# A two-layer diffusion backbone on one core: layer 0's projections written out in one order

## The chip, the core and the metric

The kernel runs on one core of a Trainium2 chip. A core has five engines that this text speaks of by their names in the profile: TensorE (PE, matmuls; its weight loads are listed as PEld), VectorE (DVE), ScalarE (ACT), GpSimd (POOL) and SyncE (SP, which here issues most DMAs). Each works through its own queue of instructions in order and waits on semaphores for the others. The metric is the time of one execution on the device in microseconds (us).

## The reference

The program computes two layers of a diffusion backbone over 1024 latent tokens and 256 context tokens of width 1024, in float32. Layer 0 is grouped-query attention (16 query heads, 4 key/value heads of 64), layer 1 is latent attention. The change touches only what layer 0 does ahead of its attention:

```
shift, scale, gate = split(silu(c) @ w_mod + b_mod, 3)          # and the same for c_ctx
h  = rms_norm(x, norm_w) * (1 + scale) + shift                   # 1024 x 1024; hc: 256 x 1024
k, v, q, g = split(h @ w_in, [256, 512, 1536])                   # 2560 columns; hc @ w_in too
q = rope(rms_norm(q per head, q_norm));  k = rope(rms_norm(k per head, k_norm))
o = softmax(q k^T / 8) v                                          # latent rows read all keys, context rows context keys
y = (o * silu(g)) @ w_out
```

## The kernel before, in words

The 1280 tokens are ten tiles of 128 rows (tiles 0 to 7 latent, 8 and 9 context), handled in five pairs. The 1024 channels are eight slices of 128, KT = 8.

*Modulation.* `mod_sections` (L197) computes silu(c) @ w_mod for one third of w_mod (a section: shift, scale or gate) and one half of the 1024 columns at a time: eight loads `mraw` of 128 x 512, and eight matmuls (L222) with 32 columns of the condition, `s32`, as the stationary operand; four neighbouring ones write four different strips of 32 partitions of one PSUM bank `pm`. `rows` copies the bank to SBUF (L228), and `end` folds it and puts it into columns A (scale) and B (shift), four channel slices for each half.

*Modulated rows.* `load_pair` (L709) loads two tiles `xt` and normalizes them (`norm_rows`: squares on ScalarE, root on GpSimd L118, scaling on VectorE). `modulate` (L278) takes two channel slices of a pair at a time: four transposes on TensorE into a PSUM bank `tp` (L288), the affine step `hmod` = tp * A + B on VectorE in two instructions of 128 x 256 (L292), the high part `hh` by a copy on ScalarE (L296), and the low part `hl` = hmod - hh on GpSimd or VectorE (L135). Each matrix is held as a high and a low part, and `mm3` (L88 to L94) forms each product from three matmuls per channel slice: high x high, low x high, high x low.

*Weights.* `load_weight` (L137) brings 1024 x 512 columns of w_in in four pieces `wraw` (L152), through three buffers, and splits each into `wa` (ScalarE, L156) and `wb` (GpSimd or VectorE, L135). There are two such pairs in a ring, so that one projection is used while the next is loaded. The order is keys and values (kv), queries in two chunks (q0, q1), gates in two chunks (g0, g1).

*Tiles.* A kv or query tile is 24 matmuls of 128x512 into one PSUM bank `mm`. `head_norm` (L776) follows: squares on ScalarE (L781), sums on VectorE, the root `h_rs` on GpSimd (L118), rope gains on VectorE and an addition on GpSimd, scaling by the root on VectorE (L800, tile `t`). Then `head_store` (L803): transposes (L808), the split, two stores.

*The order.* A scheduler of the language orders the instructions on each engine; `in_order` pins the order of TensorE alone, and only for the first modulation sections and x tiles 0 and 1. `staged` runs the transposes of a tile after the products of the next. The first half of the channel slices of tiles 0, 1 and 2 is multiplied early (`begun`), while the second half of the modulation is still being loaded. Then come kv tiles 0 to 9, q0 of tiles 0 to 9, q1 of tiles 0 to 9, the gates g0 (`gate_path`, four m of 128 gate channels, each over 512, 512 and 256 tokens), and then attention, beside which g1 is done. Between the products of the queries the modulation for later (the gate section of layer 0 and all of layer 1) is worked in, one step for every two channel slices, with its loads two steps ahead.

The pools of PSUM: three banks for products, three for transposes, two for modulation. All loads and stores go by SP's queue. The lines that set the order:

```
735    load_pair(0)                                    # pinned on TensorE
738    wkv = load_weight(w_in0, KT, 0, 512)
834    staged(range(TT), kv_stage, lambda tt, kn: head_store(kn, 4, tt, k0h, k0l, 0))
836    wq0 = load_weight(w_in0, KT, 512, 512)
856    wq1 = load_weight(w_in0, KT, 1024, 512)
857    q_chunk(0, wq0)
858    q_chunk(1, wq1)
860    wg0 = load_weight(w_in0, KT, 1536, 512)
```

## Time and profile before

| what | us |
|---|---|
| three runs | 1788.57, 1781.73, 1786.39; median 1786.39 |
| profiled execution, its own time | 1781.91 |
| span of that execution (all in the trace) | 1780.1 |
| mean granted clock of TensorE | 0.989 |
| first product of layer 0 starts | 27.19 |
| kv tile 5 done | 91.7 |
| last kv product, queries begin | 119.8 |
| queries and modulation done | 278.7 |
| gates g0 done, all that is rewritten ends | 332.5 |

The profile is one execution. Busy time is listed for each engine; a stage table gives it for stretches of the span, with the clock that TensorE was granted as a share of full speed. The list of waits says which engine stood idle at which line, and which instruction released it. In the timeline a matmul's shown duration runs over the next one's start, so the pace is read from the starts. A modulation matmul of the trace counts as x2, so x8 are four of them.

### The profile page before, as it was taken

What the parts mean: (1) busy time and instruction counts of PE and PEld (TensorE: products, weight loads), DVE (VectorE), ACT (ScalarE), POOL (GpSimd) and SP (SyncE); (2) the same over time, 40 slices, a digit from 0 to 9 for tenths busy, and PEclk for the clock granted to TensorE, in tenths of its full rate; (3) what the DMA queues carried; (4) which work ended last, traced back from release to release, by engine and by line L of the source; (5) the groups of instructions that cost most, each with busy time, mean ns of one, the idle gap of its engine ahead of it and who ended that gap; (6) DMA issues with size and microseconds to landing.
All of it is one profiled execution on the core that took longest, in us unless ns stands there. A gap on an engine that the chain in (4) does not pass through costs nothing.

```text
span 1780.1 us, 23773 instructions
## 1 busy us (share of the span) xinstructions
PE 1729.4 (97%) x8392; PEld 1224.1 (69%) x8392; DVE 1055.3 (59%) x1803; ACT 638.3 (36%) x943; POOL 978.5 (55%) x654
## 2 busy tenths in 40 slices
PE   7899999999999999999989999999999999999999
PEld 3676667885656565547878899987666666666587
DVE  3664543256777777734565667756666666666232
ACT  2431212104545444452234543331344344434410
POOL 2554431207888887873235554351677777776611
PEclk8999999999999999999999999999999999999999
DMA  8555765422242423227433776777254443533352
GB/s 288 174 157 183 233 195 164 136 71 76 66 124 66 107 71 72 72 69 216 126 109 102 207 222 167 192 210 209 51 126 103 107 106 84 119 87 74 94 170 74
DMA packets 220782, 235.01 MB, mean 132 GB/s; under 512 B 34040, under 2 KB 162792, under 8 KB 220664
## 3 DMA queue, kind: packets, MB, share of 16 engines
q1 hardware_dynamic: 220664, 233.50, 46.9%
q8 instruction: 66, 1.08, 0.3%
q14 instruction: 52, 0.43, 0.1%
HBM read 159.51 MB, written 73.63 MB: 131 GB/s over the span
## 4 chain that ended last, share of the span: by engine, by line
PE 81%; DVE 4%; POOL 3%; DMA 3%; issue 3%; ACT 1%; SPq 0%; POOLq 0%; ACTq 0%; DVEq 0%
PE st L442 21%; PE av L478 16%; PE mx L379 7%; PE mm L92 6%; PE mm L94 6%; PE mm L93 6%; PE y L92 3%; PE y L94 3%; PE y L93 3%; PE mx L384 2%; PE av L524 1%; PE pm L222 1%; DMA wraw<-in_l_w_in 1%; PE tp L808 1%; DVE wb L135 1%
## 5 line engine op out<-in xcount | busy, mean ns | idle before, releaser
L444 ACT ACTIVATE p<-st 128x1024 f32<-128x1024 f32 x328 | 335.7, 1026 | 369.4 <-PE st L442 195.8
L380 DVE TENSOR_REDUCE m<-mx 128x1 f32<-128x512 f32 x512 | 351.1, 690 | 159.0 <-PE mx L379 155.3
L465 POOL TENSOR_TENSOR acp<-acp,p 128x1024 f32<-128x1024 f32 x127 | 301.9, 2377 | 104.8 <-ACT p L444 100.7
L478 PE MATMUL av<-p,v 128*64 128x512 f32 x1312 | 296.5, 597 | 0.0
L478 PEld LDWEIGHTS av<-p,v 128*64 128x64 f32 x1312 | 88.1, 136 | 174.9 <-issue 170.1
L451 DVE TENSOR_REDUCE acd<-p 128x512 f32<-128x1024 f32 x126 | 150.3, 1234 | 23.5 <-ACT p L444 23.5
L386 DVE TENSOR_REDUCE m<-mx 128x2 f32<-128x512 f32 x144 | 99.2, 692 | 99.6 <-PE mx L384 99.0
L135 POOL TENSOR_TENSOR wb<-wraw,wa 128x512 fp32r<-128x512 f32 (+3 forms) x69 | 91.0, 1333 | 112.5 <-ACT wa L156 112.3
L465 POOL TENSOR_TENSOR acp<-acp,acd 128x1024 f32<-128x1024 f32 x63 | 149.8, 2377 | 4.2
L465 POOL TENSOR_TENSOR acp<-p 128x1024 f32<-128x1024 f32 x35 | 83.7, 2391 | 121.4 <-ACT p L444 118.0
L92 PE MATMUL mm<-wa,hh 128*128 128x512 f32 (+2 forms) x336 | 128.3, 382 | 2.5 <-ACT hh L296 2.5
L442 PE MATMUL st<-QH,KL 96*128 96x512 f32 x320 | 123.2, 392 | 0.0
L94 PE MATMUL mm<-wa,hl 128*128 128x512 f32 (+2 forms) x336 | 122.9, 367 | 0.0
L93 PE MATMUL mm<-wb,hh 128*128 128x512 f32 (+2 forms) x336 | 122.8, 366 | 0.0
L92 PE MATMUL y<-wa,oh 128*128 128x512 f32 x288 | 113.0, 392 | 2.2 <-ACT oh L642 2.2
L94 PE MATMUL y<-wa,ol 128*128 128x512 f32 x288 | 111.9, 390 | 0.6 <-DVE x_ms L116 0.6
L93 PE MATMUL y<-wb,oh 128*128 128x512 f32 x288 | 112.1, 389 | 0.0
L442 PE MATMUL st<-QA,KA 128*128 128x512 f32 x336 | 106.8, 399 | 0.9 <-ACT p L444 0.8
L442 PE MATMUL st<-QB,KB 65*128 65x512 f32 x336 | 105.5, 395 | 0.0
L379 PE MATMUL mx<-KA,QA 128*128 128x512 f32 x256 | 103.7, 410 | 0.4 <-DVE m L380 0.3
L379 PE MATMUL mx<-KH,QH 96*128 96x512 f32 x256 | 103.3, 406 | 0.8 <-DVE m L380 0.8
L92 PE MATMUL mm<-hh,wa 128*128 128x512 f32 x256 | 101.3, 396 | 0.3 <-ACT th L85 0.3
(208 smaller groups left out, 3326.4 us busy)
## 6 DMA issues: line engine op xcount, KB each, us to landing
mraw<-in_l_w_mod SPq DMA_DIRECT2D x96, 256.0 KB
wraw<-in_l_w_in SPq DMA_DIRECT2D x28, 512.0 KB
rb<-rrow SPq DMA_DIRECT2D x72, 128.0 KB
xt<-in_x SPq DMA_DIRECT2D x16, 512.0 KB
wraw<-in_l_w_out SPq DMA_DIRECT2D x16, 512.0 KB
sgd<-gth SPq DMA_DIRECT2D x32, 256.0 KB
QA<-q0h SPq DMA_DIRECT2D x32, 256.0 KB
sg<-sgd SPq DMA_DIRECT2D x64, 128.0 KB
```

The source lines that it names most:

```text
L92: pe.matmul(ps, lhsT=lh(k), rhs=rh(k), start=first and i == 0, stop=False)
L93: pe.matmul(ps, lhsT=lh(k), rhs=rl(k), start=False, stop=False)
L94: pe.matmul(ps, lhsT=ll(k), rhs=rh(k), start=False, stop=last and i == len(ks) - 1)
L135: eng.tensor_sub(lo, a, b)
L379: pe.matmul(m, lhsT=s["mq"][:, i * P:(i + 1) * P], rhs=s["mk"][:, n * 512:(n + 1) * 512], start=True, stop=True)
L380: dve.reduce_max(s["m"][:, i, n:n + 1], m, axis=AX.X)
L386: dve.reduce_max(s["m"][:, 2 * i:2 * i + 2, 2 if u["kind"] == "lat" else 0], m.rearrange("p (a b) -> p a b", a=2), axis=AX.X)
L442: pe.matmul(ps[:, n * 512:(n + 1) * 512], lhsT=lh, rhs=rf(n), start=(j == 0), stop=(j == len(prods) - 1))
L444: act.activation(p, ps, AF.Exp, scale=self.ops["scale"])
L451: dve.reduce_sum(t[:, ns], p2.rearrange("p a n -> p n a")[:, ns, :], axis=AX.X)
L465: pool.tensor_add(t, a, b)
L478: pe.matmul(s["av"][64 * n:64 * n + 64, :], lhsT=s["v"][:, kt, u["vc"]:u["vc"] + 64], rhs=p[:, n * 512:(n + 1) * 512], start=kt == kts[0], ...
```

## The change

The order of everything from the start to the first two m of g0 is now written out. A list `Plan` takes functions with a due time, sorts them and issues them with the order of all five engines pinned (TensorE, ScalarE, VectorE, GpSimd, SP). The unit of time is a quarter tile: the products of two channel slices, six matmuls.

- kv of tiles 0 to 5, then q0 of tiles 0 to 5, kv of tiles 6 to 9, q0 of tiles 6 to 9, q1 of tiles 0 to 9, m 0 and 1 of g0. m 2 and 3 follow outside of the plan by `gate_slice`, as before. For tiles 0 to 3 the first halves come first, then the second halves.
- `hmod`: of its two instructions the first one (pairs 0 to 2) or both (pairs 3 and 4) are on ScalarE as an affine activation.
- Loads: the modulation's first sections, x tiles 0 and 1, two kv weight pieces, x tiles 2 and 3, the rest of the modulation, the last two kv pieces, tables, x tiles 4 and 5, and so on. The six small loads of condition and bias rows are issued by ScalarE's queue.
- The modulation matmuls stand in groups of four. The loads of a group are issued when the group three ahead is done.
- PSUM: four banks for products, three for transposes, one for modulation. Six work buffers from the start (before: five for keys, six for queries).

The diff, cut to its core:

```diff
-    def mod_sections(which, pool_of, bufs, rowp, ps_mod, ps_tp, lag):
...
+    class ModHalf:
...
+        def load(self, k):
+            c0 = self.sec * D + self.half * 512
+            self.st[k] = self.pool_of().tile([P, 512], F32, name="mraw", tag="mraw", bufs=self.bufs)
+            sp.dma_start(self.st[k], ins[f"l{self.l}_w_mod"][k * P:(k + 1) * P, c0:c0 + 512])
+
+        def mult(self, i):
+            st = self.st
+            if i == 0:
+                st["pm"] = self.ps_mod.tile([P, 512], F32, name="pm", tag="pm")
+            for q in range(4 * i, 4 * i + 4):
+                c = 32 * (q % 4)
+                pe.matmul(st["pm"][c:c + 32, :], lhsT=s32[:, q, :], rhs=st.pop(q), start=q < 4, stop=q >= 4)
...
+    class Plan:
...
+        def at(self, t, fn, *args):
+            self.todo.append((t, len(self.todo), fn, args))
+
+        def run(self):
+            engines = mybir.EngineType
+            with tc.manual_schedule(engines={engines.PE, engines.Activation, engines.DVE, engines.Pool, engines.SP}):
+                for _, _, fn, args in sorted(self.todo, key=lambda e: e[:2]):
+                    fn(*args)
...
-    ps_mm = stP.enter_context(tc.tile_pool(name="psmm0", bufs=3, space=PSUM, reuse_waits="tile"))
+    ps_mm = stP.enter_context(tc.tile_pool(name="psmm0", bufs=4, space=PSUM, reuse_waits="tile"))
...
-    ps_mod = stT.enter_context(tc.tile_pool(name="psmod0", bufs=2, space=PSUM, reuse_waits="tile"))
+    ps_mod = stT.enter_context(tc.tile_pool(name="psmod0", bufs=1, space=PSUM, reuse_waits="tile"))
...
+    def mod_group(pair, g, t, ts, on_act, low, d=0.45):
...
+        def scale():
+            st["h"] = wk.tile([P, 512], F32, name="hmod", tag="w512")
+            for kk in range(2):
+                k = 2 * g + kk
+                dst, src = (v[:, kk * 256:(kk + 1) * 256] for v in (st["h"], st["t"]))
+                a, b = A[0][:, k, cond:cond + 1], Bv[0][:, k, cond:cond + 1]
+                if kk < on_act:
+                    act.activation(dst, src, AF.Identity, scale=a, bias=b)
+                else:
+                    dve.tensor_scalar(dst, src, a, b, op0=ALU.mult, op1=ALU.add)
...
+        plan.at(t, turn)
+        plan.at(ts, scale)
+        plan.at(ts + d, cast)
+        plan.at(ts + 2 * d, rest)
...
+    def finish_tile(nm, tt, e, nh, tabset, dst_h, dst_l, pair0, late=0):
...
+        wide = nh > 4
+        plan.at(e + 0.05, squares)
+        if nm == "kv":
+            plan.at(e + 0.7, v_store)
+        plan.at(e + 0.4, gains)
+        plan.at(e + (3.0 if wide else 2.2), scale)
+        plan.at(e + (4.5 if wide else 3.9), turn)
+        plan.at(e + (4.8 if wide else 4.2), parts)
+        plan.at(e + (5.4 if wide else 4.9), store)
...
+    def mod_loads(b):
+        if b < 8:
+            for k in range(4 * (b % 2), 4 * (b % 2) + 4):
+                halves[b // 2].load(k)
+
+    def mod_mult(b):
+
+        halves[b // 2].mult(b % 2)
+        mod_loads(b + 3)
+
+    plan.at(-50, lambda: rows.update(cond=cond_load(), cols=cols_load()))
...
+    weight("kv", 0, -48, (-47.5, -47, 5.2, 5.5), (-40, -39, 6.05, 7.2))
...
+    mod_group(1, 0, 2.6, 2.65, 1, dve, 0.1)
+    mod_group(1, 1, 3.3, 3.35, 1, dve, 0.1)
+    for tt in range(4):
+        for i in range(2):
+            plan.at(2 * tt + i, products, "kv", tt, i)
+            plan.at(8 + 2 * tt + i, products, "kv", tt, 2 + i)
+    for b, t in ((4, 1.5), (5, 2.5), (6, 4.4), (7, 5.6)):
+        plan.at(t, mod_mult, b)
...
+    for g in range(4):
+        mod_group(2, g, 12.5 + g, 12.9 + g, 1, (dve, pool)[g % 2])
+        mod_group(3, g, 25.5 + 3 * g, 26.2 + 3 * g, 2, pool)
+        mod_group(4, g, 38.5 + 2 * g, 39.2 + 2 * g, 2, pool)
...
+    slot = 16
+    for tts in (range(6), range(6, TT)):
+        for tt in tts:
+            if tt >= 4:
+                for i in range(4):
+                    plan.at(slot + i, products, "kv", tt, i)
+                slot += 4
+                kv_tile(tt, slot)
+        for tt in tts:
+            q_tile(0, tt, slot)
+            slot += 4
...
+    at_step = 47.6
+    for l, sec in ((0, 2), (1, 0), (1, 1), (1, 2)):
+        for half in range(2):
+            mh = ModHalf(l, sec, half, lambda: mp[0], 8, wk, ps_mod, ps_tp)
+            for k in range(KT):
+                plan.at(at_step + k, mh.load, k)
+            for b in range(2):
+                plan.at(at_step + 4 * b + 6.1, mh.mult, b)
...
+    for m in range(2):
+        for s0 in range(0, NT, 512):
+            slot = gate_tile(0, m, s0, slot)
+    plan.run()
...
-        gate_path(0, 0, wg0, hT, NT, ps_mm, wkg)
+        for m in range(2, 4):
+            for s0 in range(0, NT, 512):
+                gate_slice(0, 0, m, s0, min(512, NT - s0), ws["g0"], hT, ps_mm, wkg)
```

Three places of the instruction streams show what moves. The first is TensorE's queue in the first products (`mm`), where the second half of the modulation (`pm`) is worked in. Before:

```order
L92 MATMUL mm_318<-wa_246,hh_131 128x512
L222 MATMUL pm_280<-mraw_272,s32_117 32x512
L92 MATMUL mm_305<-wa_246,hh_131 128x512
...
L93 MATMUL mm_305<-wb_247,hh_131 128x512
L222 MATMUL pm_280<-mraw_274,s32_117 32x512
L94 MATMUL mm_305<-wa_246,hl_132 128x512
...
L93 MATMUL mm_318<-wb_247,hh_131 128x512
L222 MATMUL pm_280<-mraw_276,s32_117 32x512
L94 MATMUL mm_318<-wa_246,hl_132 128x512
```

and now:

```order
L94 MATMUL mm_326<-wa_169,hl_118 128x512
L198 MATMUL pm_339<-mraw_212,s32_122 32x512
L198 MATMUL pm_339<-mraw_214,s32_122 32x512
L198 MATMUL pm_339<-mraw_216,s32_122 32x512
L198 MATMUL pm_339<-mraw_218,s32_122 32x512
L92 MATMUL mm_352<-wa_169,hh_117 128x512
...
L94 MATMUL mm_352<-wa_169,hl_118 128x512
L198 MATMUL pm_339<-mraw_270,s32_122 32x512
L198 MATMUL pm_339<-mraw_272,s32_122 32x512
L198 MATMUL pm_339<-mraw_274,s32_122 32x512
L198 MATMUL pm_339<-mraw_276,s32_122 32x512
```

Before, single modulation matmuls stand between the products of tiles 0 and 1 (`mm_305`, `mm_318`) as the scheduler placed them; now four stand together behind the first twelve products of tile 0 (`mm_326`), and four more behind the first six of tile 1 (`mm_352`).

The second is TensorE's queue where keys give way to queries: `mm_1098` and `mm_787` are the last kv products, `wa_1155` and `wa_478` the high part of the query weights, `t1` the normalized keys. Before:

```order
L93 MATMUL mm_1098<-wb_247,hhc_443 128x512
L94 MATMUL mm_1098<-wa_246,hlc_444 128x512
L808 MATMUL tp_1137<-ident_70,t1_1083 128x128 x2
L92 MATMUL mm_1238<-wa_1155,hh_131 128x512
...
L94 MATMUL mm_1238<-wa_1155,hl_132 128x512
L808 MATMUL tp_1146<-ident_70,t1_1131 128x128 x2
L92 MATMUL mm_1238<-wa_1155,hh_131 128x512
```

and now:

```order
L94 MATMUL mm_787<-wa_169,hl_118 128x512
L879 MATMUL tp_859<-ident_70,t1_811 128x128 x2
L92 MATMUL mm_862<-wa_478,hh_117 128x512
...
L94 MATMUL mm_862<-wa_478,hl_118 128x512
L756 MATMUL tp_898<-ident_70,xt_551 128x128
L756 MATMUL tp_898<-ident_70,xt_553 128x128
...
L92 MATMUL mm_862<-wa_478,hh_117 128x512
...
L94 MATMUL mm_862<-wa_478,hl_118 128x512
L879 MATMUL tp_921<-ident_70,t1_883 128x128 x2
L92 MATMUL mm_924<-wa_478,hh_117 128x512
```

Before, the transposes of tile 8 stand right behind the last product of tile 9, and those of tile 9 twelve products on; now those of tile 4 stand behind tile 5, those of tile 5 24 products on, and transposes of later x tiles (`xt`) lie between.

The third is SP's queue at the start, with the semaphores that an entry waits for (one of each DMAHW number stands for a DMA slot). Before, from its 25th row:

```order
L212 DMA mraw_229<-in_l0_w_mod 128x512 [waits DMAHW7_49,PE_49]
L152 DMA wraw_248<-in_l0_w_in 128x2x512 [waits DMAHW0_49]
L152 DMA wraw_254<-in_l0_w_in 128x2x512 [waits DMAHW1_49]
L152 DMA wraw_260<-in_l0_w_in 128x2x512 [waits DMAHW2_49]
L212 DMA mraw_272<-in_l0_w_mod 128x512 [waits DMAHW3_49,PE_49]
L152 DMA wraw_266<-in_l0_w_in 128x2x512 [waits DMAHW0_49,DMAHW4_49,DVE_49,Pool_49]
L212 DMA mraw_274<-in_l0_w_mod 128x512 [waits DMAHW5_49,PE_49]
L212 DMA mraw_276<-in_l0_w_mod 128x512 [waits DMAHW6_49,PE_49]
L212 DMA mraw_278<-in_l0_w_mod 128x512 [waits DMAHW7_49,PE_49]
```

and now, from its 11th row:

```order
L726 DMA xt_167<-in_x 128x1024 [waits DMAHW7_49]
L152 DMA wraw_171<-in_l0_w_in 128x2x512 [waits DMAHW0_49]
L152 DMA wraw_173<-in_l0_w_in 128x2x512 [waits DMAHW1_49]
L190 DMA mraw_175<-in_l0_w_mod 128x512 [waits DMAHW2_49]
...
L190 DMA mraw_350<-in_l0_w_mod 128x512 [waits DMAHW3_49,PE_49]
L152 DMA wraw_420<-in_l0_w_in 128x2x512 [waits DMAHW4_49]
L152 DMA wraw_422<-in_l0_w_in 128x2x512 [waits DMAHW5_49,DVE_49,Pool_49]
L791 DMA cw_k_429<-in_rope_cos0 128x8x64 [waits DMAHW6_49]
```

Before, the fourth weight piece, which waits for VectorE and GpSimd, stands ahead of three modulation loads and of x tiles 2 and 3; now two pieces stand ahead of the modulation's second half, and the two others behind all of it.

## Rows read from the trace of the kernel before

**Rows 1.** The profile page, part 1: busy time of each engine

```profile
PE 1729.4 (97%) x8392; PEld 1224.1 (69%) x8392; DVE 1055.3 (59%) x1803; ACT 638.3 (36%) x943; POOL 978.5 (55%) x654
```

**Rows 2.** Table by stage: us, busy by engine, granted clock, DMA share, GB/s

```profile
0.00:27.20 27.20, 16.79 (x59) 5.67 (x59) 6.05 (x17) 5.58 (x10) 3.44 (x12) 0.80 0.75 262
27.20:54.20 27.00, 24.72 (x109) 13.17 (x109) 13.44 (x24) 8.82 (x16) 8.58 (x10) 0.95 0.69 229
54.20:92.00 37.80, 32.10 (x153) 25.53 (x153) 31.37 (x76) 21.39 (x46) 22.31 (x24) 0.95 0.65 206
92.00:119.80 27.80, 27.00 (x131) 22.00 (x130) 16.72 (x46) 9.32 (x24) 13.92 (x16) 1.00 0.37 106
119.80:140.00 20.20, 16.19 (x61) 12.63 (x60) 11.22 (x19) 4.72 (x9) 11.19 (x9) 0.83 0.65 208
140.00:278.70 138.70, 135.31 (x674) 92.75 (x673) 70.07 (x138) 30.04 (x54) 56.40 (x39) 1.00 0.64 198
278.70:332.50 53.80, 53.80 (x276) 46.22 (x275) 10.81 (x16) 7.62 (x14) 1.61 (x2) 0.97 0.47 138
```

**Rows 3.** List of waits, TensorE, 0 to 332.5 us: total, times, longest

```profile
PE tp L808 <- DVE t L800: 8.2, 6, 2.7
PE tp L288 <- DVE hmod L292: 5.8, 4, 3.7
```

**Rows 4.** Timeline, TensorE, 116 to 146 us: start, duration, engine, line, operation, [idle before]

```profile
122.93 0.66 PE L808 MATMUL tp<-ident,t 128*128 128x128 f32 x2 [2.74 <-DVE t L800]
...
124.67 0.63 PE L92 MATMUL mm<-wa,hh 128*128 128x512 f32 x1
...
128.51 0.63 PE L92 MATMUL mm<-wa,hh 128*128 128x512 f32 x1
...
129.45 0.39 PE L92 MATMUL mm<-wa,hh 128*128 128x512 f32 x1
...
132.89 0.39 PE L92 MATMUL mm<-wa,hh 128*128 128x512 f32 x1
```

**Rows 5.** Timeline, TensorE: the modulation matmuls, at 31 and at 151 us

```profile
30.99 1.05 PE L222 MATMUL pm<-mraw,s 128*32 128x512 f32 x2
31.96 0.50 PE L92 MATMUL mm<-wa,hh 128*128 128x512 f32 x1
...
151.01 1.07 PE L222 MATMUL pm<-mraw,s 128*32 128x512 f32 x8
```

**Rows 6.** Groups by line and shape, 27-140 us: busy, mean ns, idle

```profile
L292 DVE TENSOR_SCALAR hmod<-tp,A,B 128x256 f32<-128x256 f32 x37 | 17.8, 539 | 0.8 <-PE tp L288 0.6
L135 POOL TENSOR_TENSOR wb<-wraw,wa 128x512 fp32r<-128x512 f32 x11 | 15.4, 1407 | 15.8 <-ACT wa L156 15.8
...
L118 POOL TENSOR_TENSOR h_rs<-h_ms,mhalf 128x4 f32<-128x4 f32 x10 | 10.9, 1094 | 14.0 <-DVE h_ms L116 13.9
...
L781 ACT ACTIVATE sq<-mm 128x256 f32<-128x256 f32 x10 | 3.8, 383 | 11.5 <-PE mm L94 11.5
```

**Rows 7.** Timeline, TensorE, 278 us: the last transposes of the queries

```profile
278.04 0.63 PE L808 MATMUL tp<-ident,t 128*128 128x128 f32 x4 [1.93 <-DVE t L800]
```

**Rows 8.** Timeline, queue of SP, 0 to 60 us

```profile
18.56 0.34 SPq L212 DMA_DIRECT2D mraw<-in_l_w_mod  x1
27.62 0.37 SPq L152 DMA_DIRECT2D wraw<-in_l_w_in  x1
```

**Rows 9.** Table by stretches of 4 us, columns as in rows 2

```profile
12.00:16.00 4.00, 3.45 (x14) 1.81 (x14) 0.66 (x2) 0.00 (x0) 0.00 (x0) 0.62 0.83 287
...
20.00:24.00 4.00, 3.22 (x10) 0.49 (x6) 1.45 (x2) 1.14 (x2) 0.78 (x2) 0.60 1.03 389
24.00:28.00 4.00, 2.70 (x18) 2.36 (x19) 2.84 (x7) 1.48 (x3) 0.75 (x2) 0.83 0.10 37
```

**Rows 10.** Timeline, TensorE, 4 us: the first modulation matmuls

```profile
4.28 5.10 PE L222 MATMUL pm<-mraw,s 128*32 128x512 f32 x8 [1.39 <-DMA mraw<-in_l_w_mod]
```

**Rows 11.** Chain of waits, 0 to 500 us: start, duration, what it is

```profile
200.93 4.18 DMA wraw<-in_l_w_in
```

More of the change, by code (lines that the diff above doesn't have):

```diff
@@ L750, in hybrid_kernel @@
[L750 to L761 removed]
+    wk = stR.enter_context(tc.tile_pool(name="wk0", bufs=6, **right))
@@ L858, in hybrid_kernel, with weight, alloc, products @@
-    q_chunk(1, wq1)
-    drain(mods)
-    wg0 = load_weight(w_in0, KT, 1536, 512)
+    ws = {}
+    def weight(nm, c0, begin, loads, splits):
+        pieces, held = [], []
+        def alloc():
+            ws[nm] = load_weight(w_in0, KT, c0, 512, 2, todo=pieces)
+        plan.at(begin, alloc)
+        for i in range(4):
+            plan.at(loads[i], lambda: held.append(pieces.pop(0)()))
+            plan.at(splits[i], lambda i=i: held[i]())
+    acc = {}
+    def products(nm, tt, i):
+        if i == 0:
+            acc[nm, tt] = ps_mm.tile([P, 512], F32, name="mm", tag="mm")
+        lh, ll = h_cols(hT, tt)
+        w = ws[nm]
+        mm3(acc[nm, tt], lh, ll, lambda k: w[0][:, k, :], lambda k: w[1][:, k, :], range(2 * i, 2 * i + 2), i == 0, i == 3)
@@ new lines, in hybrid_kernel @@
+    rows = {}
+    halves = [ModHalf(0, sec, half, lambda: mp[0], 12, wk, ps_mod, ps_tp) for half in range(2) for sec in range(2)]
+    def mod_loads(b):
[7 more added lines that the diff above has]
+    for b in range(2):
+        plan.at(-49, mod_loads, b)
+    for tt in range(2):
+        plan.at(-48, x_load, tt)
```

457 lines of the change are left out of this document (253 added, 204 removed).

## The prediction

> **What bounds the kernel now.** I read the page first: TensorE is busy 97% of the span [rows 1], so only what takes time away from TensorE can move the end, and the question is where it idles or runs slowly. The table by stage [rows 2] answers that for the part that is rewritten, which ends at 332.5 us, when the first four gate channels are done. From 27.2 us on TensorE idles 27.0 - 24.7 = 2.3 us in the first products, 5.7 in the key/value tiles up to 92 us, 0.8 up to 119.8, 4.0 at the change to the queries, 3.4 in the 138.7 us of queries and modulation, and nothing in the gates: 16.2 us together. Before 27.2 us it waits for loads; there the loads bound it. The list of waits [rows 3] names what ends the idle time: mostly the transposes of normalized keys and queries (L808), which wait for VectorE, and the transposes of x (L288), which wait for a PSUM buffer that the affine step `hmod` on VectorE holds. VectorE is busy 31.4 us of 37.8 in the stage from 54.2 to 92 us [rows 2]; no other engine is so near its limit there.
>
> Two more losses are not idle time. The granted clock is 0.83 in the stage 119.8 to 140 and 0.97 in the gates [rows 2]. In the trace the products after the 2.7 us wait at 122.9 start every 3.84 / 9 = 0.427 us and later every 3.44 / 15 = 0.229 us [rows 4]: the two levels, 1.2 and 2.4 GHz. And the modulation of the second half of the channels runs matmul by matmul as its loads land: one matmul (which the trace counts as x2) holds TensorE from 30.99 to 31.96, 0.97 us, while four together (x8), which write four different strips of 32 partitions, take 1.0 us [rows 5].
>
> **The change, part by part.** The arithmetic stays: as many products, transposes and modulation matmuls. So the sum is over what surrounds them.
>
> (1) *Waits that go.* In the new order a tile's transposes stand about four quarter-tiles behind its last product (a quarter tile is 6 products, 6 x 0.229 = 1.37 us), so 5.4 us for keys and over 6 us for queries, and there is always another tile's product in between, also where keys give way to queries and queries to gates. Before, the wait at 122.9 us came because the 1.09 us root on GpSimd stood behind a 1.41 us split of query weights [rows 6], and only 12 products lay in between. I take all 16.2 us as removable, and put new waits in (4).
>
> (2) *Slow clock that goes with them.* At 119.8 to 140: 13 products at 0.427 instead of 0.229, 2.6 us. In the gates: granted 0.97 over 53.8 us, so 0.03 x 2 x 53.8 = 3.2 us at the low level, half of it lost: 1.6; it follows the 1.9 us wait at 278.0 [rows 7]. At 54.2 to 92: 0.05 x 2 x 37.8 = 3.8 us at the low level, of which part is the 3.7 us wait itself; I count 1.0. Together 5.2. The low clock of the first products (0.95 over 27.0 us, 1.4 us lost) follows the wait for loads and stays.
>
> (3) *Modulation in fours.* Of the 16 matmuls of the second half five stand alone, 5 x (0.97 - 0.25) = 3.6 us more than in fours; two and three together take about as long as four, which adds about 0.7 by the same rows. 4.3 us go, if all four loads are there. They should be: before, the queue of loads stood still from 18.56 to 27.62 us [rows 8], because the fourth weight piece waited for a buffer, and the DMA engines fell to 37 GB/s [rows 9]. Now that piece stands behind all the modulation loads. Their 4 MB follow on 7 MB, so at 0.38 MB/us they land from about 25 to 36 us, each group of four ahead of the quarter tile in which it is used (31 to 44 us by adding up the new order).
>
> (4) *New waits.* The written order holds five queues at once; a late instruction holds all behind it. The tight place is tiles 0 to 5 of the keys. Of the 40 affine pieces 28 go to ScalarE, where the nearest rows are the squares of the same shape, 0.383 us against 0.539 on VectorE [rows 6]. In the stage from the second half of tile 0 to the end of tile 5 there are 16 pieces (before, 22, all on VectorE, together with the fourth pair of x): VectorE falls from 31.4 to 31.4 - 14 x 0.54 = 23.8 us, and ScalarE rises by 8 x 0.38 = 3.1 to at most 24.5, in a stage that should now last about 31 us. So none is full, but each waits for the others in turn. By hand I followed the four queues here and found three places: the first low parts (0.8 us), the third pair's transposes, since its loads are issued only when the first pair's last transposes are done, 1.2 us, and the last quarter of tile 4, which waits for its affine step behind the three tiles' norms on VectorE, and for the low part on GpSimd, 2 us. That is 4; with what I have missed I take 5. Bounds: 0, if the engines overlap as their busy times allow, and 11.4, twice what the same kind of work loses now. For the rest, where each tile leaves the other engines half idle (VectorE 70 of 138.7 us), 1.5.
>
> The Trainium skill speaks against the affine step on ScalarE: ScalarE: Activation LUTs, section on what ACT_TABLE_LOAD costs, gives 0.186 us plus 0.83 ns per element and about 0.093 us more for each operand that is a column of per-partition values. The row agrees for the squares without such a column (0.186 + 0.213 = 0.40 against 0.383); for two columns an estimate from that page is 0.586 us, longer than VectorE's 0.539. By it ScalarE would rise 1.6 us more in the tight stage and the sum below would be at most 1.6 smaller. No row here shows such a step on ScalarE.
>
> (5) *The start.* The first product needs both first-half modulation sections. Before, 5.2 MB of loads stood ahead of their last piece, now 6.3 MB: two weight pieces come first. At 389 GB/s [rows 9] that is 2.7 us later. Against it the six small loads go to ScalarE's queue: of eight loads that may be under way four were of 4 to 12 KB there, and from 12 to 16 us the rate was 287 GB/s [rows 9], which at 389 would save about 2 us over 8 us. Then half the affine step is beside the other (0.5 us). I take 0, between -3 and +3. ScalarE's tanh now stands behind its six load issues, one of which waits for the first modulation piece, so the first modulation matmul starts later than 4.3 us [rows 10]; the loads still set the pace up to 9 us, so this costs nothing unless ScalarE is later than that.
>
> (6) *Four buffers of PSUM for products, one for modulation*: the next modulation group starts two quarter tiles behind the copy of the one before; nothing. From the first maxima on the order of TensorE's queue is unchanged, so what is gained by 332.5 us is kept to the end.
>
> Sum: 16.2 + 5.2 + 4.3 = 25.7 go, 5 + 1.5 = 6.5 come: 19.2 us. The profiled execution took 1781.9 us (span 1780.1): 1762.7. The median of the runs shown lies 4.5 us above it, which gives 1767.2. I predict 1765, between the two.
>
> **The rivals.** (A) *The tight stage gives much of it back.* Mechanism: VectorE, ScalarE and GpSimd in one written order wait in turn, each key tile's chain for the last; every wait above 2 us brings some 2 us of slow clock [rows 4]. Upper bound 11.4 us for (4), with two restarts of 2.6: the gain falls to 19.2 - 6.4 - 5.2 = 7.6, 1777. For it: GpSimd's slow pieces (1.41 and 1.09 us) lie in the chain of every key tile. Against: busy times of about 24 in 31 us.
>
> (B) *The loads' queue makes it slower.* Stores and modulation loads share SP's queue in one order, and a store waits there until its tile is split; everything behind waits too. If each of the 16 later modulation groups met its loads 2 us late, 32 us would be lost against 19 gained: 1778 + 17 = about 1795, also where queries now run with no load waited for. It decides from 1.2 us a group. Against: a group's last load is issued 3.1 quarter tiles ahead of its matmuls, at least 4.3 us, and a load of twice the size took 4.2 us from issue to landing [rows 11].
>
> (C) *The start costs its 2.7 us* and the small loads bring nothing: 16.5 us, 1768; it is inside the forecast's range.
>
> (D) *The order is held without any new wait*: 25.7 - 1.5 = 24 us, and 2 at the start: 1757.
>
> By the skill's price alone: 1766.6.
>
> **How the numbers follow.** Forecast (gain 12 to 24 us, with C): 0.68, own range 1759 to 1774. A: 0.17. B: 0.05. D: 0.10. The range that leaves out 2 in 10 reaches from D to A: 1755 to 1779. A difference of 0.5%, 8.9 us, is what can be told from no change: faster needs less than 1777.5. Forecast and D are faster throughout, and a quarter of A: 0.82; the rest of A: 0.13; B: 0.05.
>
> **What would show it.** In the changed profile: the first product at 26 to 29 us; modulation matmuls in groups of x8 with no wait for their loads; the gate's first four channels done at about 313 us instead of 332.5; TensorE idle from the first product to there about 6 us, most of it before tile 5 is done, ended by VectorE, ScalarE or GpSimd; granted clock 1.0 from 80 us on; no idle time where queries begin and where gates begin. Wrong if TensorE waits for `mraw` loads during the queries (B), if the first product comes after 31 us, if it idles over 10 us before tile 5 is done (A), or if the time after the gates is not the same as before.

## The result and the profile after

The changed kernel took 1771.74 us (median of 4 runs, 1770.01 to 1774.55), the kernel before 1785.76 (4 runs, 1781.73 to 1788.57) beside it: a ratio of 0.9925, 95% interval 0.9899 to 0.9950, so 13 to 14 us faster. The forecast was 1765, with 1755 to 1779 as its range. The gain has the right sign and some two thirds of the size; the time lies about halfway between the forecast and rival A's 1777.

The page's first line now, which answers to [rows 1]:

```profile
PE 1715.4 (97%) x8392; PEld 1218.4 (69%) x8392; DVE 1054.3 (60%) x1771; ACT 651.6 (37%) x971; POOL 985.2 (56%) x658
```

TensorE is as full as before, in a span that is 11.9 us shorter. The table by stage, with stretches that fit the new order: to the first product, the first halves of tiles 0 to 3, to the end of key tile 5, to the end of the early queries' waits, and to the end of the first four m of the gates:

```profile
0.00:27.04 27.04, 13.18 (x58) 5.50 (x58) 7.99 (x17) 7.27 (x13) 5.08 (x13) 0.83 0.92 333
27.04:48.50 21.46, 21.41 (x110) 14.12 (x111) 7.40 (x14) 7.61 (x14) 2.38 (x3) 0.89 0.78 247
48.50:85.30 36.80, 29.05 (x132) 20.81 (x130) 28.46 (x61) 22.35 (x48) 26.50 (x29) 1.00 0.59 172
85.30:112.00 26.70, 22.99 (x114) 18.67 (x114) 16.90 (x34) 12.71 (x25) 17.68 (x16) 1.00 0.18 50
112.00:317.70 205.70, 205.70 (x1044) 153.90 (x1043) 98.04 (x175) 51.58 (x98) 73.22 (x54) 1.00 0.66 200
```

Against [rows 2]: from 112 us to the end of the table TensorE never idles, through queries, later keys and gates, at full clock. What is left stands between 48.5 and 112 us: 7.75 and 3.71 us idle. And the first products run at 0.89 of the clock. The list of waits of TensorE, 0 to 340 us (total, times, longest):

```profile
PE tp L879 <- DVE t L871: 5.4, 3, 1.9
...
PE mm L92 <- ACT hh L773: 3.9, 3, 2.3
PE tp L756 <- DVE xt L740: 3.6, 3, 2.0
...
PE mm L94 <- DVE hl L776: 1.7, 1, 1.7
...
PE mm L94 <- POOL hl L776: 0.8, 2, 0.6
...
PE tp L756 <- DVE hmod L768: 0.3, 1, 0.3
```

Of the two kinds of wait in [rows 3], that for `hmod` has all but gone, from 5.8 to 0.3 us; that for the scaled tile `t` is still the largest, 5.4 us in three waits after 8.2 in six. Those for `hh`, `hl` and `xt` stand beside it; the 2.3 us of `hh` and the 2.0 of `xt` lie ahead of or at the first product. The first maxima of attention, where the queue of TensorE becomes the same in both kernels, came at 346.35 us before and come at 331.51 now, 14.8 us earlier:

```profile
331.51 0.70 PE L358 MATMUL mx<-KA,QA 128*128 128x512 f32 x2
```

A sum over the timeline says where these come from. Each row of TensorE is given the time from its start to the start of the next row, less the idle time listed there, and the rows from the first product to the first maxima are added up by kind (the second column of each kernel is the execution of a run below):

| us, first product to first maxima | before | before, again | after | after, again |
|---|---|---|---|---|
| idle | 16.1 | 15.3 | 11.3 | 12.1 |
| products | 250.2 | 247.0 | 247.9 | 247.9 |
| modulation matmuls | 25.9 | 26.0 | 19.9 | 20.1 |
| transposes and folds | 27.0 | 27.0 | 25.4 | 25.5 |
| together | 319.2 | 315.4 | 304.5 | 305.6 |

So of a mean of 12.2 us, 6 come from the modulation, 4 from waits, 1.6 from transposes, and less than 1 from products, which is where the clock shows. Why the transposes take 1.6 us less was not traced.

### The profile page after: what moved, and what is told of

It is laid out like the page before. It is cut to its first block, busy times and chain, and to the rows that moved or that the text cites. A ratio compares the mean times of both kernels' runs of the same rounds, so it can differ in the third digit from the quotient of the medians.

```text
span 1768.2 us, 23768 instructions
## 1 busy us (share of the span) xinstructions
PE 1715.4 (97%) x8392; PEld 1218.4 (69%) x8392; DVE 1054.3 (60%) x1771; ACT 651.6 (37%) x971; POOL 985.2 (56%) x658
## 4 chain that ended last, share of the span: by engine, by line
PE 85%; DMA 4%; DVE 4%; POOL 3%; issue 2%; ACT 2%; SPq 0%; ACTq 0%; POOLq 0%; DVEq 0%
PE st L421 21%; PE av L457 16%; PE mx L358 7%; PE mm L92 7%; PE mm L94 7%; PE mm L93 6%; PE y L92 3%; PE y L94 3%; PE y L93 3%; PE mx L363 2%; PE pm L198 1%; PE av L503 1%; DMA q1h<-th 1%; PE tp L879 1%; DVE wb L135 0%
## 5 line engine op out<-in xcount | busy, mean ns | idle before, releaser
L421 PE MATMUL st<-QH,KH 97*128 97x512 f32 x320 | 100.9, 396 | 0.0
```

The source lines that it names most:

```text
L421: pe.matmul(ps[:, n * 512:(n + 1) * 512], lhsT=lh, rhs=rf(n), start=(j == 0), stop=(j == len(prods) - 1))
```

## The experiments

Two measures are used below. The whole kernel's ratio to the kernel before is known to about 0.2%, 3 us. Finer is the stretch from the first product to the last fold of the modulation (`tp<-modrow,fold`) in each trace: 244.5 and 242.4 us in two executions of the kernel before, 227.6 and 228.0 in two of the changed one.

**The changed kernel again.** No edit.

> The changed kernel once more, unaltered. In its trace 14.8 us are gained by the first maxima of attention (346.4 to 331.5), but only 11.9 over the whole span: 1.1 go at the start of layer 1's rows and 1.8 at the start of its attention. Theory (the last 3 us are the scatter of loads between executions): the first maxima come within 1 us of 331.5 again, and the loss behind them differs from 3 us by a microsecond or more. Rival (the change causes it, by another layout of memory or another order of loads): the same 1 and 2 us are lost at the same places.

Ratio 0.9922 (0.9905 to 0.9938). First maxima at 332.8; the waits behind the first product agree with those of the first trace to 0.03 us each, but for one more of 0.17, and 0.7 us of the difference is a wait for a load of attention. From there to the first maxima of layer 1 this execution took 1.6 us more than the first, as scatter would have it.

**The kernel before again.** No edit.

> The kernel before, unaltered, for a second trace. From the first maxima of layer 0 to the first maxima of layer 1 its first trace took 858.9 us, the nine traces of the changed kernel and its variants, whose instructions there are the same, 860.1 to 865.0. Theory (scatter of loads between executions): another value in or near that range, 860 to 865. Rival (the change lengthens that stretch by 1 to 5 us): 858 to 860 again.

1782.83 us, one execution. From the first maxima of layer 0 to those of layer 1 it took 862.3 us: in the range of the others. The first trace of before was lucky there, and the 3 us that the changed kernel seemed to lose behind the first maxima fit scatter; with two traces of before, a part of a microsecond or two is not excluded. The second thing that this trace shows was not asked for. The wait of [rows 4] is there again, to 0.03 us, and no low clock behind it. TensorE's timeline of this run, and then its table by stretches, with the columns of the table above:

```profile
124.71 0.41 PE L808 MATMUL tp<-ident,t 128*128 128x128 f32 x2 [2.71 <-DVE t L800]
```

```profile
122.00:126.00 4.00, 1.29 (x7) 1.14 (x8) 3.10 (x3) 1.41 (x4) 3.71 (x3) 1.00 0.53 168
126.00:130.00 4.00, 4.00 (x20) 3.29 (x19) 2.65 (x6) 1.72 (x4) 0.90 (x1) 1.00 0.60 158
```

In the first execution, where the wait ended 1.8 us earlier, the same stretches had 0.52 and 0.62:

```profile
122.00:126.00 4.00, 3.07 (x9) 2.53 (x10) 3.39 (x4) 0.89 (x2) 1.91 (x2) 0.52 0.47 155
126.00:130.00 4.00, 4.00 (x13) 3.15 (x12) 0.62 (x2) 1.26 (x3) 0.07 (x1) 0.62 0.92 300
```

The wait is the program's; what the clock does behind it differs between executions.

**Key tables earlier.**

```diff
-    plan.at(7.5, tab_cos, "k")
-    plan.at(7.6, tab_sin, "k")
+    plan.at(5.95, tab_cos, "k")
+    plan.at(5.95, tab_sin, "k")
```

> GpSimd's five products of the key tables are due at 5.95 instead of 7.5, ahead of the weight splits. In the trace of the changed kernel a low part hl on VectorE takes 1.75 us at 53.47, and 0.69 elsewhere, and it ends 0.6 us behind the GpSimd product of 1.72 us that began 0.5 us ahead of it. Theory (VectorE stands still while GpSimd is in an instruction that reads SBUF): the 1.72 us wait of TensorE at 55.3 goes, unless the split that now comes later meets the same low part; first maxima 1 to 2 us earlier, 329.5 to 330.5. Rival (VectorE is only late by its queue): hl is as late as before, the wait stays, first maxima at 331.5 or later.

Ratio 0.9921 (0.9902 to 0.9941); the stretch 228.4 us. The low part took 0.68 us in place of 1.75, and the wait shrank from 1.72 to 0.22 us, as the first theory says:

```profile
55.38 0.50 PE L94 MATMUL mm<-wa,hl 128*128 128x512 f32 x1 [0.22 <-DVE hl L776]
```

Its time did not come: the first maxima, at 333.6, are in the rival's range, 1.0 us of it because the first product came later. Measured from the first product, 0.8 us were gained by 87 us, and 1.6 were lost behind: after a wait of 1.91 us the clock was low for some 3.4 us, which it was not after the same wait of 1.90 in the changed kernel. The two tables, this run's first and the changed kernel's second:

```profile
88.00:90.00 2.00, 2.00 (x7) 1.61 (x6) 1.97 (x7) 0.23 (x1) 0.53 (x1) 0.58 0.64 184
90.00:92.00 2.00, 2.00 (x6) 1.48 (x6) 0.54 (x2) 0.00 (x0) 1.18 (x2) 0.57 0.28 78
```

```profile
88.00:90.00 2.00, 2.00 (x10) 1.65 (x9) 1.94 (x7) 0.10 (x1) 0.67 (x1) 1.00 0.68 196
90.00:92.00 2.00, 2.00 (x13) 1.65 (x12) 0.43 (x1) 1.00 (x2) 1.03 (x2) 1.00 0.24 66
```

**Query weights' low parts on VectorE.**

```diff
-            ws[nm] = load_weight(w_in0, KT, c0, 512, 2, todo=pieces)
+            ws[nm] = load_weight(w_in0, KT, c0, 512, 1 if nm == "q0" else 2, todo=pieces)
```

> The low parts of the first query weights, half on GpSimd and half on VectorE, are all on VectorE: GpSimd loses four splits of about 1.3 us, VectorE gets them for 0.68 us each. Theory (a GpSimd split that starts 0.07 us ahead of a key tile's scaling by the root holds VectorE for its whole length: 64.87 and 64.94, 85.65 and 85.72): the scaling takes 0.45 instead of 1.47 us, the waits of 1.67 and 1.90 us go, first maxima 2 to 3.5 us earlier, 328 to 329.5. Rival (VectorE is full in this stage, 28 of 37 us): 2.7 us more work make its waits longer, first maxima at 332 to 334.

Ratio 0.9915 (0.9899 to 0.9931), the stretch 227.1 us. The two scalings took 0.41 and 0.43 us instead of 1.47, as the first theory says; the wait of 1.67 us went, and that of 1.90 became 1.13. VectorE's timeline at the first of them:

```profile
65.12 1.82 DVE L135 TENSOR_TENSOR wb<-wraw,wa 128x512 fp32r<-128x512 f32 x2
66.87 0.41 DVE L871 TENSOR_TENSOR t<-t,h_rs 128x256 f32<-128x256 f32 x1
```

But the two splits ahead of it are what VectorE took over, so that scaling ended only 0.3 us earlier, measured from the first product. The rest of the 1.67 us was covered by a slower TensorE: 62 to 68 us was at 0.72 of the clock. And waits for `hh` and `t` of 0.95 and 0.75 us came at tiles behind, so idle time fell only from 11.3 to 9.6 us. The first maxima, at 332.6, are in the rival's range, 1.2 us of it because the first product came later.

**All affine pieces on VectorE.**

```diff
-                if kk < on_act:
-                    act.activation(dst, src, AF.Identity, scale=a, bias=b)
-                else:
-                    dve.tensor_scalar(dst, src, a, b, op0=ALU.mult, op1=ALU.add)
+                dve.tensor_scalar(dst, src, a, b, op0=ALU.mult, op1=ALU.add)
```

> All affine pieces are on VectorE again, as before the change; the rest as in the changed kernel. Theory of the prediction (VectorE is the tight engine from 48 to 85 us; it gets 8 pieces of 0.54 us there, 4.3 us): first maxima 2 to 5 us later, 333.5 to 336.5. Rival (the handing over from ScalarE to VectorE to ScalarE costs as much as the second engine saves, 0.56 + 0.6 us against 2 x 0.54): first maxima within 1 us of 331.5.

Ratio 0.9924 (0.9907 to 0.9940), the stretch 229.4 us: 1.4 to 1.8 longer, between the two. First maxima at 334.3, but the first product came 1.0 us later too. The affine step on ScalarE is worth under 2 us in the trace and nothing that the times show.

**Transposes a quarter tile later.**

```diff
-        plan.at(e + (4.5 if wide else 3.9), turn)
-        plan.at(e + (4.8 if wide else 4.2), parts)
-        plan.at(e + (5.4 if wide else 4.9), store)
+        plan.at(e + (5.4 if wide else 4.9), turn)
+        plan.at(e + (5.7 if wide else 5.2), parts)
+        plan.at(e + (6.3 if wide else 5.9), store)
```

> The transposes of normalized keys and queries, their split and their stores are due one quarter tile later (0.9 for queries). Measured from the first product to the last fold of the modulation, two executions of the changed kernel took 227.6 and 228.0 us, the kernel before 244.5. Theory (the waits of 1.7, 1.9 and 1.8 us are short of cover by less than the 1.37 us of a quarter tile, and nothing else is late behind them): 4 to 5.4 us fewer, 222.5 to 224 us, no low clock behind the first products. Rival (VectorE is the bound from 48 to 112 us, so that its lateness only moves to the next low part or affine step): at most 1.5 us fewer, with new waits at products (hh, hl).

Ratio 0.9906 (0.9891 to 0.9920), the stretch 223.5 us, with no low clock behind the first products. The time is the first theory's, its reason only half. The three waits fell from 5.4 to 0.4 us, but waits for `hmod` (1.6 and 0.3) took part of it back: idle time fell from 11.3 to 8.6. The rest came with products, 3.2 us less, against 1.7 more for the transposes. About 1 us of that is the clock, ahead of anything that the edit moves: 6 of the first products started at the lower pace, against 11 in the changed kernel.

**Modulation matmuls apart.** The groups of the second half are dissolved (due times of the rows behind shift by 0.15):

```diff
+        for k in range(2 * i, 2 * i + 2):
+            one()                                  # one modulation matmul
+            pe.matmul(ps, lhsT=lh(k), rhs=w[0][:, k, :], start=k == 0, stop=False)
+            one()
+            pe.matmul(ps, lhsT=lh(k), rhs=w[1][:, k, :], start=False, stop=False)
+            pe.matmul(ps, lhsT=ll(k), rhs=w[0][:, k, :], start=False, stop=False)
...
-    for b, t in ((4, 1.5), (5, 2.5), (6, 4.4), (7, 5.6)):
-        plan.at(t, mod_mult, b)
```

> The 16 modulation matmuls of the second half of the channels stand one by one between product matmuls instead of in four groups of four. Theory of the prediction (one alone holds TensorE 0.97 us, four in neighbouring strips together 1.0): 16 x 0.97 - 4 x 1.0 = 11.5 us more TensorE time in the first products, of which up to 3 are taken from the waits behind them: first product to last fold 236 to 239.5 us against 227.6 and 228.0. Rival (a matmul alone costs its 512 columns, 0.25 us, and the 0.97 were a wait for its load): within 2 us of 228.

Ratio 1.000 (0.9986 to 1.0013): with this the whole gain is gone. It is more than the change undone, for before it only five of the 16 stood alone: the modulation matmuls now take 32.4 us, 6.5 more than in the kernel before. The stretch is 243.6 us, above the 236 to 239.5 that were expected; the profiled execution was the slowest of ten, 9 us above their median. Of the 16 us more than in the changed kernel 12.5 are in the modulation matmuls, at 0.98 us each (37.33 - 36.35):

```profile
36.35 1.04 PE L996 MATMUL pm<-mraw,s 128*32 128x512 f32 x2
37.33 0.50 PE L1006 MATMUL mm<-wb,hh 128*128 128x512 f32 x1
```

The prediction's price holds. The rest is products, 3.9 us more, in part at low clock, in the first products and at 100 to 112 us behind a wait of 1.95.

**Only TensorE's order written.**

```diff
-            with tc.manual_schedule(engines={engines.PE, engines.Activation, engines.DVE, engines.Pool, engines.SP}):
+            with tc.manual_schedule(engines={engines.PE}):
```

> The plan pins the order of TensorE alone; the scheduler orders VectorE, ScalarE, GpSimd and SP. Theory A (the written order of the other queues keeps their work behind what TensorE needs): waits grow by 3 to 10 us, first product to last fold 231 to 238 us. Theory B (it is TensorE's order with its distances that brings the gain; in the written order of GpSimd a split stands right behind the addition that VectorE waits for, and this order has it too by chance or not): 225 to 230 us.

Ratio 0.9929 (0.9914 to 0.9944), the stretch 229.8 us: in theory B's range, 2 us longer than the changed kernel. Theory A's 3 to 10 us of further waits did not come. Idle time is the same, 11.1 us, but in fewer and longer waits, the longest of them this:

```profile
84.53 0.79 PE L94 MATMUL mm<-wa,hl 128*128 128x512 f32 x1 [4.59 <-POOL hl L776]
```

Products take 2.1 us more, with 50 to 56, 68 to 74 and 80 to 88 us partly at low clock. So TensorE's order with its distances brings nearly all. Whether the written order of the four other queues is worth the 2 us is not shown: they are products at low clock in one trace, two executions of the kernel before differ by 3.1 us in their products, and the ratios don't tell the two kernels apart.

**All keys first.**

```diff
-    for tts in (range(6), range(6, TT)):
+    for tts in (range(TT),):
...
-        mod_group(3, g, 25.5 + 3 * g, 26.2 + 3 * g, 2, pool)
-        mod_group(4, g, 38.5 + 2 * g, 39.2 + 2 * g, 2, pool)
+        mod_group(3, g, 17.5 + 1.5 * g, 18.2 + 1.5 * g, 2, pool)
+        mod_group(4, g, 25.5 + 1.5 * g, 26.2 + 1.5 * g, 2, pool)
```

(and the norms of x tiles 6 to 9, the first query weights and the query tables moved to fit)

> All ten key and value tiles ahead of the queries, as before the change, with x tiles 6 to 9, their affine pieces and the query weights' splits moved to fit; the rest as in the changed kernel. Theory (a key tile brings other engines more work per quarter tile than a query tile, with GpSimd at about 10 of 11 us per pair of tiles, so that four more tiles in a row add 1 to 2 us of waits each): first product to last fold 232 to 236 us. Rival (the distances alone matter, and which tiles come first doesn't): 226 to 229 us.

Ratio 0.9923 (0.9907 to 0.9940), the stretch 230.6 us, between the two ranges. Idle time is 11.95 us, 0.6 more than in the changed kernel, and the longest wait comes from a scaling that this edit had put late:

```profile
77.19 0.91 PE L756 MATMUL tp<-ident,xt 128*128 128x128 f32 x3 [2.60 <-DVE xt L740]
```

Behind it the clock was at 0.75 in 74 to 80 us, and products and modulation take 0.9 us more each. No tile among the four further ones waits 1 to 2 us, so the first theory falls: half the queries between the keys is worth nothing that this run can show.

**First weights behind the modulation's loads.**

```diff
-    weight("kv", 0, -48, (-47.5, -47, 5.2, 5.5), (-40, -39, 6.05, 7.2))
+    weight("kv", 0, -48, (-45.35, -45.3, 5.2, 5.5), (-40, -39, 6.05, 7.2))
```

> The first two weight pieces for keys and values are loaded behind the 16 modulation loads of the first half of the channels instead of ahead of their second section. In eight executions of the order of the changed kernel, or kernels that differ from it only behind the start, the first product came at 27.0 to 29.3 us, the affine chain of the second section ending last. Theory of the prediction (the 1 MB ahead costs 2.7 us at 389 GB/s): the modulation ends up to 2.7 us earlier, and the first product comes at 25 to 26.5 us, unless the weights are then late themselves. Rival (the loads as a whole set the start, since 7 MB must land for the first product whatever their order): 27 to 29 us, now behind the weights.

Ratio 0.9933 (0.9916 to 0.9949); the first product at 30.55 us, later than in any other. Neither theory: the second section's matmuls ran at 20.57, as in the changed kernel (20.19), because the transposes of x stand ahead of them and wait for VectorE's scaling. Then TensorE waited 3.2 us for the copy of its rows, which stood on VectorE behind weight splits whose load was late:

```profile
20.57 2.57 PE L198 MATMUL pm<-mraw,s 128*32 128x512 f32 x16
26.34 1.87 PE L219 MATMUL tp<-fold,modrow 128*128 128x2 f32 x8 [3.19 <-DVE modrow L202]
```

**Two versions that join the findings.** Later transposes, earlier tables, norms of x tiles 4 and 5 earlier, and other splits of the first query weights:

```diff
-    weight("q0", 512, 7, (7.1, 8.1, 9.1, 12.5), (12.1, 13.1, 14.1, 20.5))
+    weight("q0", 512, 7, (7.1, 8.1, 9.1, 10.5), (9.3, 10.3, 13.6, 18.5))
...
-        x_norm(tt, 8.6 + 0.3 * (tt - 4), (0, 0.4, 1.5))
+        x_norm(tt, 7.35 + 0.75 * (tt - 4), (0, 0.5, 2.3 - 0.45 * (tt - 4)))
```

> Four edits to the changed kernel: transposes one quarter tile later (as in the run with later transposes: 223.5 us from the first product to the last fold), the key tables at 5.95 (which took away 1.5 us of wait at the second halves), the norms of x tiles 4 and 5 two steps earlier (waits of 1.1 and 0.5 us), the first query weights' splits earlier, where GpSimd is free. Theory (each of these waits is late work on VectorE, held by a GpSimd instruction or standing in its queue, and what is moved finds room): 219 to 222 us, whole kernel 1764 to 1769. Rival (the stage from 48 to 85 us is full on VectorE, ScalarE and GpSimd together, so that a wait moves on): 222.5 to 225 us, 1768 to 1772.

Ratio 0.9912 (0.9896 to 0.9927), 1768.64 us; the stretch 224.4 us, with 5.9 us idle. Waits shrank as the first theory has it, but one of 2.0 us was left at 62.0 us, the clock was at 0.72 in 62 to 68 us, and the stretch is the rival's, while the whole kernel's time fits both. In the second version the low parts stand on VectorE between gains and scaling, and the norms' scaling comes earlier:

```diff
+    weight("q0", 512, 7, (7.1, 8.1, 9.1, 10.7), (10.5, 13.15, 15.85, 18.55))       # all low parts on VectorE
+        x_norm(tt, 7.35 + 0.75 * (tt - 4), (0, 0.5, 1.55 - 0.7 * (tt - 4)))
```

> The four edits of the run before, with two alterations: the first query weights' low parts are all on VectorE, each piece between a key tile's gains and its scaling, where VectorE otherwise waits for the root on GpSimd; and the scaling of x tiles 4 and 5 stands ahead of the next affine piece. Theory (what is left of the waits, 2.0 and 1.5 us, comes from VectorE instructions held by GpSimd splits at 59.2 and 68.1 us, and the 2.0 us wait brought a low clock that took 1.7 us more): no wait above 1.2 us behind the first product, no low clock behind 35 us, 219 to 222 us from the first product to the last fold, the whole kernel 1762 to 1767. Rival (VectorE is full in this stage, and 2.7 us more work on it is waited for in other places): 223 to 226 us, 1767 to 1771.

Ratio 0.9902 (0.9885 to 0.9919), 1767.53 us; the stretch 220.4 us, 7 less than the changed kernel, with 4.6 us idle. The stretch is the first theory's and the whole kernel's time the rival's, by half a microsecond. Both signs of the first theory failed: one affine piece is late, a wait of 2.1 us, and 68 to 74 us is at 0.72.

```profile
68.09 0.66 PE L756 MATMUL tp<-ident,xt 128*128 128x128 f32 x4 [2.14 <-DVE hmod L768]
```

It is the fastest of the family by its trace. By the whole kernel's time its interval meets the changed kernel's (0.9899 to 0.9950), so the times alone don't separate the two.

## Why the prediction was right, and where not

The sum had 19.2 us: 5.2 by the clock, 4.3 by modulation, and 9.7 by waits, less what comes new. On the mean of two executions each, 12.2 us came by the first maxima: less than 1 by the clock, 6 by modulation, 4 by waits, and 1.6 by transposes, which the sum didn't have. That the time lay in the range is in part luck: what modulation and transposes brought more made up for part of what clock and waits brought less.

*(1) Waits that go: held behind 112 us, in part ahead of it.* Behind 112 us no wait is left, and that for `hmod` went as foretold. But waits for `t` did not all go: one of 1.90 us, at 87.24, is where queries begin, which the distances were to rule out.

*(2) Slow clock that goes with them: the wrong kind of term.* 5.2 us were read from one execution's clock. The second execution has nearly the same waits, 15.3 us for 16.1, and loses 3.1 us less in its products. And after the change the first products start at low clock and stay there longer. What is left on the mean of two executions each is under 1 us in the products, and perhaps part of the 1.6 in the transposes.

*(3) Modulation in fours: held, and somewhat more.* 4.3 us were foretold; in the first products the matmuls take 4.0 us in place of 8.9, as groups of x8 with no wait for a load:

```profile
32.17 1.06 PE L198 MATMUL pm<-mraw,s 128*32 128x512 f32 x8
33.16 0.50 PE L92 MATMUL mm<-wa,hh 128*128 128x512 f32 x1
```

Another us comes from the 16 later groups. The run with matmuls apart shows the price of one alone again.

*(4) New waits: the term that was mis-sized.* 5 us were taken for the tight stage and 1.5 behind it; 7.6 came up to 85.3 us, inside the bound of 11.4, and 3.7 behind. VectorE's busy share was judged rightly (23.8 of 31 us foretold, 28.5 of 36.8 from 48.5 to 85.3). What the sum of busy times can't show is that VectorE stands still beside GpSimd, and that this counts as busy: some 6 of the 28.5 us, an estimate from ten instructions in VectorE's timeline against the shortest of their kind and shape. The three longest waits for keys and queries on TensorE's timeline, [idle before]:

```profile
66.56 0.41 PE L879 MATMUL tp<-ident,t 128*128 128x128 f32 x2 [1.67 <-DVE t L871]
...
87.24 0.44 PE L879 MATMUL tp<-ident,t 128*128 128x128 f32 x2 [1.90 <-DVE t L871]
...
109.89 0.63 PE L879 MATMUL tp<-ident,t 128*128 128x128 f32 x4 [1.81 <-DVE t L871]
```

VectorE's timeline, the instructions behind such waits, and two of the same kind and shape elsewhere:

```profile
50.69 0.69 DVE L776 TENSOR_TENSOR hl<-hmod,hh 128x512 fp32r<-128x512 f32 x1 [0.68 <-ACT hh L773]
...
53.47 1.75 DVE L776 TENSOR_TENSOR hl<-hmod,hh 128x512 fp32r<-128x512 f32 x1
...
64.94 1.47 DVE L871 TENSOR_TENSOR t<-t,h_rs 128x256 f32<-128x256 f32 x1 [0.62 <-POOL t L866]
...
85.72 1.47 DVE L871 TENSOR_TENSOR t<-t,h_rs 128x256 f32<-128x256 f32 x1 [0.88 <-POOL t L866]
...
91.07 0.43 DVE L871 TENSOR_TENSOR t<-t,h_rs 128x256 f32<-128x256 f32 x1 [1.10 <-POOL t L866]
```

GpSimd's timeline at the same places:

```profile
52.95 1.72 POOL L797 TENSOR_TENSOR cw_k<-cw_k,w_k 128x512 f32<-128x512 f32 x1
...
64.87 2.68 POOL L135 TENSOR_TENSOR wb<-wraw,wa 128x512 fp32r<-128x512 f32 x2
...
85.65 1.26 POOL L135 TENSOR_TENSOR wb<-wraw,wa 128x512 fp32r<-128x512 f32 x1
```

A low part takes 0.69 us alone and 1.75 where a GpSimd product began 0.5 us ahead of it; a scaling takes 0.43 us alone and 1.47 where a split began 0.07 us ahead. The low part ends 0.55 us behind the GpSimd product, the scaling at 85.72 ends 0.28 behind the split: each does its work when that one is done. The Trainium skill, SBUF — State Buffer, section Who interferes with whom, says that a VectorE instruction with two inputs in SBUF contends with a GpSimd instruction that reads SBUF, and calls the ports that they share an exclusive lock; the trace agrees, by 1.0 us more on 0.43. The written order makes this regular. GpSimd's addition `t` releases both VectorE's scaling and, by standing next in its own queue, the split; GpSimd is 0.07 us quicker each time. It could be read ahead of the change, in the wait of [rows 4], which the prediction put down to the late root and the short distance. VectorE's scaling there, in the kernel before, and GpSimd's split, 0.06 us ahead of it:

```profile
121.30 1.48 DVE L800 TENSOR_TENSOR t<-t,h_rs 128x256 f32<-128x256 f32 x1 [0.90 <-POOL h_rs L118]
```

```profile
121.24 2.67 POOL L135 TENSOR_TENSOR wb<-wraw,wa 128x512 fp32r<-128x512 f32 x2
```

The waits of 1.72, 1.67, 1.90 and 1.81 us make 7.1 of the 11.3 us. In each, one VectorE instruction takes 1.0 us longer beside GpSimd; the rest of the 1.67 and the 1.90 lies in the chain ahead of it. Moving the tables took the first wait away, but for 0.22 us. Moving the splits brought both scalings down to 0.4 us, but the second wait only to 1.13, and the first was mostly covered by a slower TensorE. The fourth stands behind a scaling of x, VectorE's timeline first and then GpSimd's:

```profile
107.39 1.76 DVE L740 TENSOR_SCALAR xt<-xt,x_rs 128x1024 f32<-128x1024 f32 x1 [2.86 <-POOL x_rs L118]
109.07 0.68 DVE L871 TENSOR_TENSOR t<-t,h_rs 128x512 f32<-128x512 f32 x1
```

```profile
104.30 1.28 POOL L866 TENSOR_TENSOR t<-t,t 128x512 f32<-128x512 f32 x1
105.54 1.30 POOL L776 TENSOR_TENSOR hl<-hmod,hh 128x512 fp32r<-128x512 f32 x1
106.80 0.56 POOL L118 TENSOR_TENSOR x_rs<-x_ms,mhalf 128x1 f32<-128x1 f32 x1
107.32 1.28 POOL L776 TENSOR_TENSOR hl<-hmod,hh 128x512 fp32r<-128x512 f32 x1
```

The addition that the scaling of `t` needs was done at 105.58, but the written order of VectorE holds it behind the scaling of x, which waits 2.86 us for a root that stands behind a low part on GpSimd, and then takes 1.76 us beside the next low part (0.75 elsewhere). That is the prediction's own mechanism, a late instruction that holds all behind it. This fourth wait was only read; no run tried it by itself.

The affine step on ScalarE took 0.563 us, beside 0.538 on VectorE:

```profile
L766 ACT ACTIVATE hmod<-tp,B,A 128x256 f32<-128x256 f32 x27 | 14.4, 563 | 18.4 <-PE tp L756 15.7 <-DVE A L230 1.7 <-DVE hss L852 1.0
...
L768 DVE TENSOR_SCALAR hmod<-tp,A,B 128x256 f32<-128x256 f32 x11 | 5.9, 538 | 6.6 <-ACT hmod L766 6.6
```

The prediction had taken the squares' 0.383; the estimate from the Trainium skill, ScalarE: Activation LUTs, section What ACT_TABLE_LOAD costs, was 0.586, and the measurement is near it. The difference to the squares, 0.18 us on 8 pieces, is 1.4 us of ScalarE's time.

*(5) The start: held as a number, not as a reason.* The first product came at 27.04 us; over all traces it is 27.2 and 28.4 before, and 27.0 to 29.3 with the new order of loads. Not the megabytes of the weights set it but a chain behind the loads of x: norm on VectorE, transposes, second section, fold, affine step.

*(6) The rest is kept to the end: held.* The 3 us that seem lost there fit scatter, 858.9 and 862.3 us from maxima to maxima before, 860.1 to 865.0 over the others.

Of the signs, the first product, the groups of x8, the full clock from 80 us on and the loads came as written. The first four m of the gates were done at 317.7 us, not at about 313, and TensorE idled 11.3 us up to there, not 6.

Of the rivals, A comes nearest to what the tight stage did, though 7.6 us of waits by the end of tile 5 stay under the 10 that were its sign. Its slow clock didn't come in this kernel; that every wait above 2 us brings one, as A has it, the runs don't bear out: it came behind 1.91 us in one run, and not behind 2.71 us in the kernel before. B is out: no matmul of the later modulation waits for its loads. (Its sum, 1778 + 17, doesn't follow: 32 us lost on the forecast give 1797.)

No run tried the four banks for products, the six buffers, or the small loads on ScalarE's queue by themselves, so what these bring stays open.

## What to carry to other kernels

Price small-column matmuls by how they stand: four that write neighbouring strips cost as much as one alone, 1.0 us, which brought 6 of 12.2 us here. When work is written out for several engines, look where VectorE and GpSimd are released by the same instruction, and give GpSimd nothing long there: here it made 0.43 us into 1.47, and the sum of busy times didn't show it. A wait can be read from one trace, but the clock behind it can't: count it as a range.

## What the runs showed that was not expected

Most waits of one program agree between executions to a few hundredths of a microsecond (in the changed kernel all but one of 0.17 us, in the kernel before not one of 1.01 and one of 1.27); the granted clock behind a wait of 1.9 to 2.7 us doesn't. Behind 2.7 us the clock was at 0.52 in one execution and at 1.00 in another, behind 1.9 us at 0.58 and at 1.00. Shorter waits are not safe either. In the run with the query weights' low parts on VectorE, the products behind two waits of 1.14 and 0.49 us started every 0.43 us; in the changed kernel the same two waits stand at 61.69 and 62.51, and the clock stayed at 1.00:

```profile
63.17 0.33 PE L756 MATMUL tp<-ident,xt 128*128 128x128 f32 x1 [1.14 <-DVE xt L740]
64.00 0.65 PE L756 MATMUL tp<-ident,xt 128*128 128x128 f32 x3 [0.49 <-DVE xt L740]
...
64.87 0.63 PE L93 MATMUL mm<-wb,hh 128*128 128x512 f32 x1
65.30 0.63 PE L94 MATMUL mm<-wa,hl 128*128 128x512 f32 x1
```

And an idle total says little of what the clock costs: with TensorE's order alone written, 11.1 us in six waits came with products 2.1 us longer than 11.3 us in eleven waits, in one trace.
